# Four seven-product k pairs instead of three in two more FFN column groups, and two sums of squares taken at fixed later steps

## The chip, the cores and the metric

The kernel runs on one core of a Trainium2 chip. The metric is the device time of one execution in microseconds (us); less is better. Engines are called by the profile's names: PE (TensorE matmul), PEld (its weight load), DVE (VectorE), ACT (ScalarE), POOL (GpSimd) and SP (SyncE, which issues most transfers).

## The reference, cut to what matters

A trunk of two pre-norm residual layers over x of 1 x 256 x 2048 in float32. Layer 0 mixes with sliding-window attention and an mLSTM, layer 1 with forgetting attention (FoX); each is followed by the same feed-forward network (FFN) with 5632 hidden columns:

```python
def swiglu(xn, w_gate, w_up, w_down):
    return (jax.nn.silu(xn @ w_gate) * (xn @ w_up)) @ w_down

for layer in range(DEPTH):
    xn = rms_norm(h, norm_mix[layer])
    mix = swa_mlstm_mixer(...) if layer % 2 == 0 else forgetting_attention_mixer(...)
    h = h + mix
    h = h + swiglu(rms_norm(h, norm_ffn[layer]), w_gate[layer], w_up[layer], w_down[layer])
return rms_norm(h, norm_final)
```

The change touches the two products with `w_gate` and `w_up`, in both layers, and the step from layer 0's FFN to layer 1, where `rms_norm` needs the mean of the squares of h.

## The kernel before, in words

**Float32 products.** Every float32 operand is split into a high part (a cast to fp32r) and a low part (the operand less the high part). A product is then three matmuls: high·high, high·low and low·high (`three`, L531). For weights ACT makes the cast and DVE the subtraction: `split_chunk` (L187, L188) for a chunk as it is loaded, 128 x 1024, and `split_plain` (L356, L357) for anything else. The split weights lie in eight slots that are used in turn.

**Tiles.** The 256 rows are two row tiles. k (2048) is walked in eight pairs of 128-row slices, numbered 0 to 7. The 5632 hidden columns are eleven groups (0 to 10) of 512. `ffn` (L637) does groups 0–2, 3–6 and 7–10 (`PARTS`), and after each of these parts the down projection over the hidden columns made so far, in two halves of 1024 output columns (`n0` = 0 and 2).

**Pairs.** `pair_group` (L539) computes one group: gate and up for 512 columns, both row tiles, over the eight k pairs in a given order. There are two kinds of pair. A *plain* pair (kind 0) has 2 matrices x 2 slices x 2 row tiles, 8 products of three matmuls: 24 matmuls. A *seven-product* pair (kind 1) takes the two slices, the two row tiles and the two matrices as a 2 x 2 by 2 x 2 block product and does it with seven block products (as Strassen and Winograd do): 21 matmuls. Its weight sums are made by DVE (L607 to L610, four instructions of 128 x 512) before they are split: one loaded chunk, the second half of the other, and two blocks of sums are cast and subtracted. The matching sums of x are made once per layer and kept: for pairs 1, 3 and 5 in `sx`, for pair 7 (`FOURTH`) in `x4` and in unused parts of xh and xl (`sums_x`, L640).

**Order of pairs.** Most groups use `ORDER`, which makes pairs 1, 3 and 5 seven-product; the groups in `DENSE` use `HEAVY`, which makes 1, 3, 5 and 7 so and begins with one. `DENSE` is (4, 8), in both layers.

**Banks.** PSUM has two sets of four banks. A group's plain sums take one set, the seven products' shared sums (`prods`, four banks) the other, and the next group swaps them. At a group's end `combine` (L553) copies or adds the four prods into c, and L665 adds the four plain banks. So the next group's products wait for L665, and its plain sums for `combine`.

**What sets the order.** The kernel is traced under a scheduler that puts each engine's instructions in an order of its own. Beyond that, a list `todo` ties a job to a step: `run_due` runs it after the weights of the given position of a group have been split.

**Layer 0's end.** The last down projection's second half (`n0` = 2) follows that of `n0` = 0. When an output quarter n of 512 columns is done, `close` (L727) adds it to h (`add_out`, L370, and L758), turns it and splits it into the x of layer 1, and takes its squares. Quarter 0 is turned by DMA: `split_turned` copies it to 16-bit planes in a box (L315), issues four transposes (L317), and its second half, put in `todo` at step 5, copies them back (L322) and scales and splits them (L361 on ACT, L362 on DVE). Quarters 1 to 3 are turned on PE and split likewise. The squares (`square_sum`, L240) are two ACT instructions of 128 x 512 per quarter (L245), and are issued right after a quarter's turn. `r1 = rstd("m1")` needs all of them, at the start of layer 1.

Of the kernel before, what the change touches and what calls it, by code (L numbers as in the profile page):

```python
# [35 lines left out]
ORDER = ((0, 0), (1, 1), (0, 2), (1, 3), (0, 4), (1, 5), (0, 6), (0, 7))  # L36
HEAVY = ((1, 1), (0, 0), (1, 3), (0, 2), (1, 5), (0, 4), (1, 7), (0, 6))
FOURTH = 7
DENSE = (4, 8)
DOWN = {  # L40
    6: ((0, 0), (1, 1), (0, 2), (1, 3), (0, 4), (0, 5)),
    8: ((0, 0), (1, 1), (0, 2), (1, 3), (0, 4), (1, 5), (0, 6), (0, 7)),
# [9 lines left out]
W_RAWS = 4  # L52
LATER = (6, 10, 3, 5)
LATER_DOWN = (5, 6)
RAWS = 4
P_JOIN = 4
COLD = 9
# [18 lines left out]
def trunk(  # L76
# [51 lines left out]
    def load_raw(w, k0, c0, n, pool=wr, bufs=4, raws=None):  # L128
        if raws:
            raw = raws.pop(0)  # L130
            raws.append(raw)
        else:
            raw = pool.tile([P, CK, NB], F32, tag="raw", name="raw", bufs=bufs)
        loaded[0] = nc.sync.dma_start(
            raw[:, :, 0:n], w[k0 * P : (k0 + CK) * P, c0 : c0 + n].rearrange("(k p) n -> p k n", p=P)
        )
        return raw
# [46 lines left out]
    def split_chunk(raw, n):  # L184
        hi, lo = slot()
        for k in (slice(0, 1), slice(1, CK)) if any(raw is f for f in fine) else (slice(0, CK),):
            latest[0] = nc.scalar.copy(hi[:, k, 0:n], raw[:, k, 0:n])  # L187
            nc.vector.tensor_tensor(  # L188
                out=lo[:, k, 0:n], in0=raw[:, k, 0:n], in1=hi[:, k, 0:n].bitcast(F32), op=ALU.subtract
            )  # L190
        return hi, lo
# [48 lines left out]
    def square_sum(key, n):  # L240
        if n == 0:
            sums[key] = sm.tile([P, NT, 4], F32, tag="ss", name="ss")
        for t in range(NT):
            junk = sm.tile([P, NB], BF16, tag="junk", name="junk", bufs=1)
            nc.scalar.activation(  # L245
                junk, h[:, t, n * NB : (n + 1) * NB], AF.Square, accum_out=sums[key][:, t, n : n + 1]
            )
# [34 lines left out]
    def split_scaled(idx, n, extra=None, joined=None):  # L282
        for half in range(2):
            if joined is None:
                pt = pm.tile([P, 2, NT, P], F32, tag="pm", name="pt")
                for i in range(2):
                    k = 4 * n + 2 * half + i
                    for t in range(NT):
                        nc.tensor.transpose(pt[:, i, t, :], h[:, t, k * P : (k + 1) * P], ident)
            else:  # L290
                pt = joined[:, 2 * half : 2 * half + 2, :].rearrange("p i (t q) -> p i t q", t=NT)
            for i in range(2):
                k = 4 * n + 2 * half + i
                src = pt[:, i, :, :].rearrange("p t q -> p (t q)")
                split_gained(xh[:, k, :], xl[:, k, :], src, idx * KT + k)
            pair = 2 * n + half
            if extra is not None and (pair in mixed_of(ORDER) or pair == FOURTH):
                sh, sl, x4, pool = extra

                def copies(full):  # L300
                    for i in range(2):
                        g = gT[:, idx * KT + 2 * pair + i : idx * KT + 2 * pair + i + 1]
                        nc.scalar.mul(full[:, i, :], pt[:, i, :, :].rearrange("p t q -> p (t q)"), g)

                if pair == FOURTH:
                    sums_of(pool, rooms(xh), rooms(xl), copies, x4=x4)
                else:
                    j = mixed_of(ORDER).index(pair)
                    sums_of(pool, sh[:, j, :, :], sl[:, j, :, :], copies)

    def split_turned(idx, n, flat, turned, extra=None):
        planes = flat.bitcast(U16).rearrange("p (b t n) -> p b t n", b=2, t=NT)
        hu = h[:, :, n * NB : (n + 1) * NB].bitcast(U16).rearrange("p t (n b) -> p t n b", b=2)
        for b in range(2):
            nc.scalar.copy(planes[:, b, :, :], hu[:, :, :, b])  # L315
            for t in range(NT):
                nc.sync.dma_start_transpose(turned[:, b, :, t, :], planes[:, b, t, :])  # L317

        def join():
            ju = flat.bitcast(U16).rearrange("p (n b) -> p n b", b=2)  # L320
            for b in range(2):
                nc.scalar.copy(ju[:, :, b], turned[:, b, :, :, :].rearrange("p k t q -> p (k t q)"))  # L322
            split_scaled(idx, n, extra, flat.rearrange("p (k s) -> p k s", k=4))

        return join

    def turn(src, dst):
        planes = dst.rearrange("p k s -> p (k s)").bitcast(U16).rearrange("p (b t n) -> p b t n", b=2, t=NT)
        turned = src.rearrange("p t n -> p (t n)").bitcast(U16).rearrange("p (b k t q) -> p b k t q", b=2, t=NT, q=P)
        su = src.bitcast(U16).rearrange("p t (n b) -> p t n b", b=2)  # L330
        for b in range(2):
            nc.scalar.copy(planes[:, b, :, :], su[:, :, :, b])
        for b in range(2):
            for t in range(NT):
                nc.sync.dma_start_transpose(turned[:, b, :, t, :], planes[:, b, t, :])

        def join():
            du = dst.rearrange("p k s -> p (k s)").bitcast(U16).rearrange("p (n b) -> p n b", b=2)
            for b in range(2):
                nc.scalar.copy(du[:, :, b], turned[:, b, :, :, :].rearrange("p k t q -> p (k t q)"))  # L340

        return join

    def scrap(fp, n):
        if n % 2 == 0:
            box = fp.tile([P, 4, NB], F32, tag="c", name="box", bufs=1)
            halves = box[:, 0:2, :], box[:, 2:4, :]
        elif n == 3:
            halves = [fp.tile([P, 3, NB], F32, tag=f"sd{i}", name="box", bufs=1)[:, 0:CK, :] for i in range(2)]
        else:  # L350
            halves = [fp.tile([P, CK, NB], F32, tag="raw", name="box", bufs=RAWS) for _ in range(2)]
        flat, turned = (a.rearrange("p a n -> p (a n)") for a in halves)
        return flat, turned.bitcast(U16).rearrange("p (b k t q) -> p b k t q", b=2, t=NT, q=P)
# [13 lines left out]
    def add_out(acc, n):  # L367
        for t in range(NT):
            o = h[:, t, n * NB : (n + 1) * NB]
            nc.vector.tensor_tensor(out=o, in0=acc[t], in1=o, op=ALU.add)  # L370
# [165 lines left out]
    def bank(par, name):  # L536
        return pm.tile([P, NB], F32, tag="pm", name=name) if par else pa.tile([P, NB], F32, tag="acc", name=name)

    def pair_group(fp, par, lhs, sums, mats, order, todo=(), halves=None, inner=None, raws=None):  # L539
# [32 lines left out]
        for pos, (kind, pair) in enumerate(order):  # L572
# [21 lines left out]
            if first:  # L594
                prods = [bank(1 - par, "prod") for _ in range(4)]
            ra, rb = (load_raw(w, k0, c0, NB, fp, W_RAWS if halves else RAWS, raws) for w, c0 in mats)
            hg, lg = split_chunk(ra, NB)
# [39 lines left out]
    def ffn(layer, fp, sx, x4, sd, key, todo, idx_next=None, key_next=None, finish=None):  # L637
# [8 lines left out]
        for g0, g1 in zip(PARTS, PARTS[1:]):  # L646
# [3 lines left out]
            for g in range(g0, g1):  # L650
# [6 lines left out]
                    [(w_gate[layer], g * NB), (w_up[layer], g * NB)],  # L657
                    HEAVY if g in DENSE else ORDER,
                    todo,
                )  # L660
                todo = []
# [59 lines left out]
                todo = [(MID if g < g1 - 1 else MID_DOWN, join)]  # L721
# [5 lines left out]
            def close(acc, n):  # L727
                if not end:
                    add_out(acc, n)
                elif idx_next is None:  # L730
                    finish(acc, n, gf)
                else:
                    add_out(acc, n)
                    if n < 1:
                        todo.append((LATER_DOWN[n], split_turned(idx_next, n, *scrap(fp, n))))
                    else:
                        split_scaled(idx_next, n)
                    square_sum(key_next, n)

            gf = None  # L740
            wd = w_down[layer][4 * g0 * P : 4 * g1 * P, :]
            for n0 in (0, 2):
# [9 lines left out]
                todo = []  # L752
# [44 lines left out]
    with tc.tile_pool(name="ev", bufs=1) as ev:  # L797
# [223 lines left out]
        with tc.tile_pool(name="mp", bufs=1) as mp:  # L1021
# [39 lines left out]
            todo = [(AHEAD_M[m], turn(src, dst)) for m, (src, dst) in enumerate(((qm, qmt), (km, kmt)))]  # L1061
# [92 lines left out]
    with tc.tile_pool(name="od", bufs=1) as od:  # L1154
# [56 lines left out]
        def sums_of_x(j, pair):  # L1211
            def make():
                box = od.tile([P, 12, P], F32, tag="tt", name="box")
                sums_of(od, sx[0][:, j, :, :], sx[1][:, j, :, :], whole(xh, xl, pair), box=box)

            return make

        todo = [(p, sums_of_x(j, pair)) for p, j, pair in [(1, 1, 3), (3, 2, 5), (6, 0, 1)]]
# [15 lines left out]
        for i in range(4):  # L1234
# [23 lines left out]
            elif i < 3:  # L1258
                n = NB if i == 1 else VT
# [117 lines left out]
```

## Time and profile before

| what | us |
|---|---|
| median of 3 runs | 2077.42 |
| lowest and highest | 2076.88 and 2078.46 |
| profiled execution | 2078.39 |
| span of the profile | 2076.7 |

The profile is of one execution, with times in us from the start of its span. A row of the timeline gives the start, the duration, the engine, the kernel's line, the operation, what it writes and reads, the shapes, and how many such instructions in a row were merged; what stands in brackets is the engine's idle time before it and the instruction that ended it. A row of the windows gives each engine's busy time in a stretch. Instructions of one engine overlap a little, so that the duration of a row is longer than the distance to the next start. 512 hidden columns take about 41 us in every FFN group, and there are 22 of them.

### The profile page before, as it was taken

To read this page: it belongs to the slowest core of one execution; us is meant where nothing else is said; L and a number is where in the kernel's file an instruction comes from. 1 tells how busy PE (TensorE), PEld (TensorE's weight loads), DVE (VectorE), ACT (ScalarE), POOL (GpSimd) and SP (SyncE) were. 2 spreads that over 40 slices of the span, in tenths; PEclk is the share of its full clock that TensorE was granted. 3 is DMA by queue.
4 is the path that set the end of the run, shared out by engine and by line. 5 is a ranking of instruction groups with operands and counts; after the bars stand their busy time and mean duration, and the time that the engine had idled before them with its cause. 6 is when DMAs were issued, how large, how long until landed. Compare 5 with 4: busy or idle time off the path is not lost.

```text
span 2076.7 us, 26845 instructions
## 1 busy us (share of the span) xinstructions
PE 2064.6 (99%) x9461; PEld 1712.5 (82%) x9461; DVE 1833.4 (88%) x2391; ACT 1379.3 (66%) x1752; POOL 45.8 (2%) x66
## 2 busy tenths in 40 slices
PE   9999999999999999999999999999999999999998
PEld 7878888888888888888888888888888888888887
DVE  6788769999999999999899678689999999999995
ACT  6777678664676656667677676687655677556763
POOL 1010000000000000000000001000000000000000
PEclk9999999999999999999999999999999999999999
DMA  8566577666567666665676766586756667756664
GB/s 290 171 216 190 189 244 239 212 213 197 187 216 236 210 195 220 225 208 185 206 211 210 224 201 181 160 274 209 233 183 214 213 187 231 232 183 203 207 221 149
DMA packets 309574, 434.86 MB, mean 209 GB/s; under 512 B 106412, under 2 KB 114624, under 8 KB 309312
## 3 DMA queue, kind: packets, MB, share of 16 engines
q1 hardware_dynamic: 307088, 426.27, 65.1%
q0 software_dynamic: 1632, 5.80, 0.8%
q8 instruction: 74, 1.21, 0.2%
q10 hardware_dynamic: 720, 1.09, 0.2%
q14 instruction: 60, 0.49, 0.1%
HBM read 408.68 MB, written 2.12 MB: 198 GB/s over the span
## 4 chain that ended last, share of the span: by engine, by line
PE 89%; DVE 4%; DMA 3%; ACT 2%; issue 2%; SPq 0%; POOLq 0%; POOL 0%; ACTq 0%; DVEq 0%
PE acc L532 19%; PE acc L533 19%; PE acc L534 19%; PE acc L223 5%; PE acc L222 5%; PE acc L224 5%; PE prod L532 5%; PE prod L533 5%; PE prod L534 5%; DVE lo L188 1%; DMA raw<-in_w_in_odd_dram 1%; ACT hi L187 1%; DMA raw<-in_w_down_dram 1%; PE p L386 1%; PE po L487 0%
## 5 line engine op out<-in xcount | busy, mean ns | idle before, releaser
L187 ACT CAST hi<-raw 128x1024 fp32r<-128x1024 f32 (+3 forms) x652 | 657.5, 1027 | 406.6 <-PE acc L534 183.3
L188 DVE TENSOR_TENSOR lo<-raw,hi 128x1024 fp32r<-128x1024 f32 (+3 forms) x652 | 767.3, 1195 | 133.7 <-ACT hi L187 130.3
L533 PE MATMUL acc<-lo,xh 128*128 128x512 f32 x1296 | 504.6, 389 | 0.0
L534 PE MATMUL acc<-hi,xl 128*128 128x512 f32 x1296 | 501.7, 389 | 0.0
L532 PE MATMUL acc<-hi,xh 128*128 128x512 f32 x1296 | 487.4, 390 | 0.0
L534 PEld LDWEIGHTS acc<-hi,xl 128*128 128x128 f32 x1296 | 243.3, 188 | 50.5
L533 PEld LDWEIGHTS acc<-lo,xh 128*128 128x128 f32 x1296 | 243.3, 188 | 50.4 <-issue 0.2
L532 PEld LDWEIGHTS acc<-hi,xh 128*128 128x128 f32 x1296 | 243.3, 188 | 50.4 <-issue 0.2
L356 ACT CAST hi<-raw 128x512 fp32r<-128x512 f32 x212 | 172.8, 819 | 83.0 <-PE acc L534 60.0
L357 DVE TENSOR_TENSOR lo<-raw,hi 128x512 fp32r<-128x512 f32 x212 | 198.8, 940 | 6.3 <-ACT hi L356 6.3
L533 PE MATMUL acc<-lo,mh 128*128 128x512 f32 x466 | 180.8, 389 | 0.0
L534 PE MATMUL acc<-hi,ml 128*128 128x512 f32 x466 | 179.7, 389 | 0.0
L532 PE MATMUL acc<-hi,mh 128*128 128x512 f32 x466 | 171.0, 390 | 1.0 <-ACT hi L187 1.0
L356 ACT CAST hi<-t 128x1024 fp32r<-128x1024 f32 x99 | 104.1, 1051 | 69.2 <-PE prod L534 42.2
L357 DVE TENSOR_TENSOR lo<-t,hi 128x1024 fp32r<-128x1024 f32 x99 | 121.2, 1224 | 10.5 <-ACT hi L356 10.2
L223 PE MATMUL acc<-lo,mh 128*128 128x512 f32 (+1 forms) x322 | 126.3, 392 | 0.0
L222 PE MATMUL acc<-hi,mh 128*128 128x512 f32 (+1 forms) x322 | 125.8, 391 | 0.0
L224 PE MATMUL acc<-hi,ml 128*128 128x512 f32 (+1 forms) x322 | 123.7, 391 | 0.0
L532 PEld LDWEIGHTS acc<-hi,mh 128*128 128x128 f32 x466 | 87.3, 188 | 20.5 <-ACT hi L187 2.6
L533 PEld LDWEIGHTS acc<-lo,mh 128*128 128x128 f32 x466 | 87.5, 188 | 18.3 <-DVE lo L188 0.2
L534 PEld LDWEIGHTS acc<-hi,ml 128*128 128x128 f32 x466 | 87.5, 188 | 18.2
L223 PE MATMUL acc<-lo,xh 128*128 128x512 f32 (+3 forms) x288 | 99.9, 347 | 0.2 <-DVE lo L188 0.2
(362 smaller groups left out, 3219.7 us busy)
## 6 DMA issues: line engine op xcount, KB each, us to landing
raw<-in_w_gate_dram SPq DMA_DIRECT2D x176, 512.0 KB, 4.4
raw<-in_w_up_dram SPq DMA_DIRECT2D x176, 512.0 KB, 4.6
raw<-in_w_down_dram SPq DMA_DIRECT2D x176, 512.0 KB, 5.3
raw<-in_w_in_odd_dram SPq DMA_DIRECT2D x88, 512.0 KB, 5.1
raw<-in_w_in_even_dram SPq DMA_DIRECT2D x51, 512.0 KB, 5.2
raw<-in_w_out_even_dram SPq DMA_DIRECT2D x32, 512.0 KB, 5.4
raw<-in_w_out_odd_dram SPq DMA_DIRECT2D x32, 512.0 KB, 4.9
hr<-in_w_in_even_dram SPq DMA_DIRECT2D x12, 512.0 KB, 4.6
```

Source lines behind the costliest of these rows:

```text
L187: latest[0] = nc.scalar.copy(hi[:, k, 0:n], raw[:, k, 0:n])
L188: nc.vector.tensor_tensor(out=lo[:, k, 0:n], in0=raw[:, k, 0:n], in1=hi[:, k, 0:n].bitcast(F32), op=ALU.subtract)
L222: nc.tensor.matmul(o, ah[:, ts], hi, start=(k == 0), stop=False)
L223: nc.tensor.matmul(o, ah[:, ts], lo, start=False, stop=False)
L224: nc.tensor.matmul(o, al[:, ts], hi, start=False, stop=(k == k_all - 1 and cs.stop == n))
L356: nc.scalar.copy(dst_h, src)
L357: nc.vector.tensor_tensor(out=dst_l, in0=src, in1=dst_h.bitcast(F32), op=ALU.subtract)
L386: nc.tensor.matmul(pq[j % 2][:, j // 2, :], q_of(j, b), k_of(j)[:, 0:cols], start=True, stop=True)
L532: nc.tensor.matmul(o, ah, hi, start=start, stop=False)
L533: nc.tensor.matmul(o, ah, lo, start=False, stop=False)
L534: nc.tensor.matmul(o, al, hi, start=False, stop=stop)
```

## The change

`DENSE` takes in groups 5 and 9, so that in both layers groups 4, 5, 8 and 9 have four seven-product pairs and four plain ones, in the order of `HEAVY`. Groups 5 and 9 lose a plain pair 7 and gain a seven-product pair 7; each has six DVE instructions more (one subtraction of 128 x 1024, one of 128 x 512, four sums of 128 x 512), two ACT casts more (128 x 1024 and 128 x 512) and three matmuls fewer. The loads are the same.

At layer 0's end the squares of quarters 0 and 1 are no longer issued at once, but put in `todo` for steps 2 and 6 of the second half of the down projection. Quarters 2 and 3 stay as they were, as does layer 1's end, which has no such sums (`idx_next` is None there).

```diff
-DENSE = (4, 8)
+DENSE = (4, 5, 8, 9)
...
 LATER_DOWN = (5, 6)
+SQUARES = (2, 6)
...
                     else:
                         split_scaled(idx_next, n)
-                    square_sum(key_next, n)
+                    if n < 2:
+                        todo.append((SQUARES[n], lambda: square_sum(key_next, n)))
+                        todo.sort(key=lambda it: it[0])
+                    else:
+                        square_sum(key_next, n)
```

In ACT's order, the first of quarter 0's two squares stays ahead of the box copies, with a weight cast between, and the second follows them; quarter 1's two come after the casts of the following weights. Lines of the changed kernel are one higher than before from L55 on, and five higher after `close`.

## The prediction

> **What bounds the kernel now.** I read the page first: the busy line, the granted clock, the chain that ended last. Its columns are busy time, share of the span and count.
>
> ```profile
> PE 2064.6 (99%) x9461; PEld 1712.5 (82%) x9461; DVE 1833.4 (88%) x2391; ACT 1379.3 (66%) x1752; POOL 45.8 (2%) x66
> ...
> PEclk9999999999999999999999999999999999999999
> ...
> PE 89%; DVE 4%; DMA 3%; ACT 2%; issue 2%; SPq 0%; POOLq 0%; POOL 0%; ACTq 0%; DVEq 0%
> ```
>
> The reader is to see that TensorE has 12 us of a 2077 us span without work, at the full clock in every slice, and that VectorE at 88% is the only other engine near a limit. So two things can move the time: fewer matmuls, or a VectorE that is late for the matmuls left. The shares are averages, so I then cut layer 0's second half into windows at the first matmul of each group. Columns: stretch, length, then busy (count) of PE, PEld, DVE, ACT and POOL, granted clock, DMA share, GB/s.
>
> ```profile
> 552.30:593.10 40.80, 40.80 (x181) 33.79 (x180) 38.55 (x50) 28.60 (x32) 0.00 (x0) 1.00 0.66 213
> 593.10:634.60 41.50, 41.50 (x184) 34.36 (x183) 40.26 (x51) 29.67 (x32) 0.00 (x0) 1.00 0.69 222
> 634.60:676.10 41.50, 41.50 (x185) 34.37 (x184) 39.63 (x50) 27.55 (x30) 0.00 (x0) 1.00 0.63 206
> ...
> 841.40:882.80 41.40, 41.40 (x184) 34.31 (x183) 38.89 (x49) 28.79 (x33) 0.00 (x0) 1.00 0.67 218
> 882.80:924.30 41.50, 41.50 (x184) 34.35 (x184) 40.50 (x52) 28.39 (x31) 0.00 (x0) 1.00 0.65 212
> 924.30:966.00 41.70, 41.70 (x185) 34.53 (x184) 39.77 (x47) 28.73 (x31) 0.00 (x0) 1.00 0.70 225
> 966.00:1010.80 44.80, 43.24 (x193) 34.78 (x192) 40.86 (x55) 28.34 (x44) 0.00 (x0) 1.00 0.46 137
> ```
>
> They are groups 4, 5 and 6, then 9, 10 and both halves of the last down projection. PE is busy for the whole of every group, and only the last window, where layer 0 ends, has matmuls that wait. Group 4, which has four seven-product pairs already, takes 40.80, and group 5 beside it takes 41.50. VectorE leaves only 1 to 2.5 us free in each.
>
> **The change part by part.** (a) *Matmuls.* A seven-product pair is 21 matmuls, a plain pair 24, so each of groups 5 and 9 loses three. The price is the difference of the two rows: 41.50 − 40.80 = 0.70 by edges rounded to 0.1; by pitch, 41.50/183 = 0.2267 us a matmul, so 0.68. Two groups in two layers: **−2.72 us**. This is on the path that sets the end, because PE has no idle time there.
>
> (b) *Casts and sums.* A plain pair has two casts and two subtractions of 128x1024. A seven-product pair has three and one half as wide, and four sums of 512. So VectorE gets one more 1024 subtraction and five more 512 instructions a group, ScalarE one cast of each width. The input sums of pair 7 exist already, since groups 4 and 8 use them.
>
> ```profile
> 970.47 2.36 DVE L188 TENSOR_TENSOR lo<-raw,hi 128x1024 fp32r<-128x1024 f32 x2
> ...
> 975.73 0.70 DVE L609 TENSOR_TENSOR raw<-raw,t 128x512 f32<-128x512 f32 x1
> 976.46 0.69 DVE L610 TENSOR_TENSOR raw<-raw 128x512 f32<-128x512 f32 x1
> ...
> 983.83 0.68 DVE L607 TENSOR_TENSOR t<-raw 128x512 f32<-128x512 f32 x1
> 984.42 0.69 DVE L608 TENSOR_TENSOR t<-raw 128x512 f32<-128x512 f32 x1
> ```
> ```profile
> L187 ACT CAST hi<-raw 128x1024 fp32r<-128x1024 f32 x13 | 13.5, 1053 | 9.0 <-PE acc L534 4.6 <-issue 1.7 <-DMA raw<-in_w_gate_dram 1.4
> ...
> L356 ACT CAST hi<-raw 128x512 fp32r<-128x512 f32 x3 | 1.9, 617 | 0.3 <-PE acc L534 0.3
> ```
>
> Instructions overlap, so I count from start to start. L608 starts 0.59 after L607; I take 0.60. Two subtractions take 2.36 together and one alone 1.23 (the 649.89 row below), so they start 1.13 apart. So 1.13 + 5 × 0.60 = **4.13 us of VectorE** a group. ScalarE's 1.05 + 0.62 lie beside matmuls: it is busy for 29.67 of 41.50. The loads are the same, 973 SP instructions before and after; only their order changes, and at layer 0's end the 272-wide loads, which are needed first, go ahead of some 512-wide ones. POOL's work is unchanged. I cost these at nothing; no matmul in the windows before the last one waits for a transfer.
>
> Group 5 now opens its second product bank at its 49th matmul, 593.1 + 48 × 0.2267 = 604.0. The bank is free after the second of group 4's additions in this row:
>
> ```profile
> 600.79 1.89 DVE L665 TENSOR_TENSOR c<-acc,c 128x512 f32<-128x512 f32 x3
> ```
>
> The first of its three is the second bank's, done by about 601.5: 2.5 us of cover, so nothing as long as VectorE is not later than that.
>
> (c) *What the 4.13 does to the matmuls.* VectorE's 4.13 more and PE's 0.68 less make it 4.81 later against PE, less the idle time that it can fill. The cover is the lead of a written low half over its first matmul. These are the lowest leads that I found, each with the writer and the first reader:
>
> ```profile
> 610.92 2.37 DVE L188 TENSOR_TENSOR lo<-raw,hi 128x1024 fp32r<-128x1024 f32 x2
> ...
> 615.12 0.39 PE L533 MATMUL acc<-lo,xh 128*128 128x512 f32 x1
> ```
> ```profile
> 649.89 1.23 DVE L357 TENSOR_TENSOR lo<-raw,hi 128x1024 fp32r<-128x1024 f32 x1
> ...
> 655.46 0.39 PE L533 MATMUL prod<-lo,sx 128*128 128x512 f32 x1
> ...
> 900.14 2.37 DVE L188 TENSOR_TENSOR lo<-raw,hi 128x1024 fp32r<-128x1024 f32 x2
> ...
> 904.83 0.39 PE L533 MATMUL acc<-lo,xh 128*128 128x512 f32 x1
> ...
> 1711.17 2.37 DVE L188 TENSOR_TENSOR lo<-raw,hi 128x1024 fp32r<-128x1024 f32 x2
> ...
> 1715.73 0.39 PE L533 MATMUL acc<-lo,xh 128*128 128x512 f32 x1
> ```
>
> Of each pair of subtractions the first counts: it ends 1.23 after the row's start. Group 5: 615.12 − 612.15 = 2.97, in mid-group, when about half of the extra work is done. Group 6: the 649.89 row ends at 651.12, 4.34 ahead of 655.46. Group 10: 904.83 − 901.37 = 3.46. Layer 1's group 6: 1715.73 − 1712.40 = 3.33. Against 4.81 that leaves waits of 0.5, 1.35 and 1.5 if no idle is filled, and none if 1.5 is. VectorE's idle is 1.24 in group 5, 1.87 in group 6, 2.51 in group 9. For groups 5/6 of both layers and 9/10 of layer 1 I take a quarter of the worst, 0.35 each: **+1.0** (0 to 2.5: 0.5 and 1.5 for the two group 6, and 0.5 for layer 1's group 10, taken like layer 0's group 6). Layer 0's group 10 runs into (d) and is counted there.
>
> (d) *Layer 0's end.* Here VectorE has no lead. It works without a pause from the row below, 21 rows of the timeline, to the 976.46 row above, which ends at 977.15:
>
> ```profile
> 951.44 0.69 DVE L607 TENSOR_TENSOR t<-raw 128x512 f32<-128x512 f32 x1 [0.91 <-DMA raw<-in_w_down_dram]
> ```
> ```profile
> DVE lo L188 <- ACT hi L187: 2.1, 2, 1.3
> ```
>
> VectorE's idle in the windows of 9, 10 and the first down half is 2.51 + 1.00 + 1.93 = 5.44. The last row above, waits of VectorE from 841.4 to 966 (total, times, longest), is of a kind that stays, as a cast must come first; I leave out 1.8 for it. 3.6 of 4.81 is filled, and layer 0's end comes **+1.2** later (0 to 4.8).
>
> (e) *The squares.* Rows of ScalarE there, two waits of 972 to 993, and the transposes (first and last issue; time to landing):
>
> ```profile
> 973.47 0.63 ACT L245 ACTIVATE junk<-h 128x512 bf16<-128x512 f32 x1 [0.23 <-DVE h L370]
> ...
> 974.66 2.00 ACT L315 COPY box<-h 128x1024 uint16<-128x1024 uint16 x2 [0.47 <-DVE h L370]
> 976.56 0.63 ACT L245 ACTIVATE junk<-h 128x512 bf16<-128x512 f32 x1
> ...
> 977.19 1.03 ACT L187 CAST hi<-raw 128x1024 fp32r<-128x1024 f32 x1
> 978.13 0.62 ACT L245 ACTIVATE junk<-h 128x512 bf16<-128x512 f32 x1
> ...
> 980.21 0.62 ACT L245 ACTIVATE junk<-h 128x512 bf16<-128x512 f32 x1
> ...
> 981.77 0.82 ACT L361 ACTIVATE xh<-pt,gT 128x256 fp32r<-128x256 f32 x2
> 982.49 2.57 ACT L322 COPY box<-box 128x1024 uint16<-128x1024 uint16 x2
> ```
> ```profile
> PEld acc L532 <- ACT hi L187: 1.4, 2, 0.7
> ...
> PE prod L532 <- DVE xl L362: 1.0, 1, 1.0
> ```
> ```profile
> L317 SPq DMA_TRANSPOSE box<-box x4: 1202/1239/1259, 975.7 to 979.6; - x4
> ...
> DMA to landing us min/median/max: 2.4/2.5/2.5
> ```
>
> All four squares stand among the copies and casts that the waiting matmuls need. In the changed order quarter 0's two stay in this stretch; quarter 1's two, 978.13 and 980.21, go behind the casts, 1.25 us off the chain. The 977.19 cast also goes ahead of the box copies and fills the 0.47 pause, so the first L361 could start up to 1.7 sooner (1.25 + 0.47). But that cast takes about 0.9 until its successor starts, 0.4 more than the pause, so the box copies and the transposes come 0.4 later: the last lands at 979.6 + 2.5 + 0.4 = 982.5, where its copy back now starts near 983.7 (the second of the two from 982.49), a gain of 1.2 at most. I take **−1.1** (−1.7 to 0).
>
> Sum: −2.72 + 1.0 + 1.2 − 1.1 = **−1.6 us**. The profiled execution took 2078.39, 1.69 of it around the span, and is 0.97 over the median of the runs, so I take the difference from the median: 2077.42 − 1.6 = **2075.8 us**.
>
> **Rivals.** *R1, VectorE becomes the bound* (the other side: slower). Its place is group 5 to 6, 9 to 10 and layer 0's end; its price 4.81 per group; it decides where the idle isn't filled. With nothing filled, 2.5 + 4.8 = 7.3 comes back against 3.8 saved: 2077.42 + 3.5 = 2080.9. Half of it is the turning point. For it: 40.26 + 4.13 is more than group 5's 40.8. Against: four seven-product pairs in group 4 fit in 38.55, and the groups behind leave idle. If the squares' gain fails with it, 2082.0. *R2, every cover holds:* leads of 3 to 4.3 plus the idle are enough: −2.72 − 1.1 gives 2073.6; with the squares' best, 2073.0. *R3, the squares are worth nothing*, as L362 waits for VectorE, not for ScalarE (the 1.0 row): −2.72 + 2.2 gives 2076.9. That the move is only half made is in (e) already. *R4, the added sums don't overlap:* the four hang on one another, and L610 right behind L609 starts 0.73 later (975.73, 976.46), so 5 × 0.73 + 1.23 = 4.88, 0.75 more at each of four places: 2075.8 + 3.0 = 2078.8. Against it, L607 and L608 start 0.59 apart at 0.68 each. The Trainium skill ("VectorE: DVE Perf Modes", section The DRAIN you can't avoid) states such a rule: the next instruction doesn't start until the pipe is empty, unless it isn't held, when it starts earlier. By the rule R4 would hold; the rows 0.59 apart fit its exception.
>
> **How the numbers follow.** Forecast 0.42, R1 0.25, R2 0.18, R3 0.10, R4 0.05. A measurement of this kernel can tell 0.2%, 4.2 us, from no change: under 2073.3 is faster, over 2081.6 slower. Forecast, R3 and R4 lie within, as does R2 but for its low end (0.08 faster). Of R1, half (0.13) lies over the bound: 0.7 more than its 2080.9, by the squares' failure or one more wait, is enough. Same: 0.79. The range goes from R2's low end, 2073.0, to R1's high end, 2082.0.
>
> **What would show it.** In the changed kernel the windows of groups 5 and 9 take 40.8 us with PE busy throughout, and VectorE's busy time there is some 4 us higher with six instructions more. PE's waits for L188 and L357 in groups 5, 6, 9 and 10: under 1 us in sum for R2, about 1 for the forecast, over 2 for R1. At layer 0's end quarter 1's squares stand behind the first L361, the first of these starts ahead of 981.77 less 1.36, and the last window is near 45; at 48 or more R1 holds. L607 to L610 more than 0.7 apart would show R4. A clock under 1.00, or matmuls waiting for a load, would be outside all of this and make the prediction wrong.

## The result: 10.7 us slower, and the profile after

The changed kernel takes 2087.85 us (median of 4 runs, 2087.45 to 2088.21) against 2077.15 before on the same chip: a ratio of 1.0049, with a 95% interval of 1.0036 to 1.0061. The prediction was 2075.8, with a range up to 2082.0. The profiled execution took 2088.18, its span is 2086.3, 9.6 longer than before.

The busy line of the page, and the windows of layer 0's groups 5, 6, 9, 10 and of the last half of its down projection, cut at the first matmuls of the changed kernel's groups:

```profile
PE 2067.5 (99%) x9449; PEld 1709.8 (82%) x9449; DVE 1849.0 (89%) x2415; ACT 1385.5 (66%) x1760; POOL 42.9 (2%) x66
```
```profile
593.70:636.50 42.80, 41.73 (x182) 33.74 (x181) 41.51 (x52) 29.70 (x33) 0.00 (x0) 1.00 0.70 203
636.50:678.10 41.60, 41.60 (x183) 34.09 (x182) 40.51 (x52) 29.04 (x32) 0.00 (x0) 1.00 0.68 220
843.90:886.20 42.30, 41.63 (x182) 33.81 (x181) 41.25 (x52) 29.22 (x33) 0.00 (x0) 1.00 0.68 203
886.20:929.00 42.80, 42.15 (x184) 34.12 (x183) 41.43 (x53) 29.07 (x32) 0.00 (x0) 1.00 0.68 219
970.40:1017.90 47.50, 44.48 (x194) 36.30 (x194) 42.05 (x54) 30.19 (x48) 0.00 (x0) 0.96 0.47 141
```

The page still says 99% and 89%; it doesn't show what happened. The windows do: group 5 has fewer matmuls and takes 42.8 instead of 41.5, and so it goes in group 10, which the diff doesn't touch. VectorE's busy time grew by 1849.0 − 1833.4 = 15.6, against 16.5 forecast (4 × 4.13).

This table has the length in us of the groups that differ most, start to start of the groups' first matmuls, as in the windows; the columns behind "after" are experiments of the next section. In the kernel of "load" PE's order mixes the end of group 8 with the start of group 9, so group 9 is taken there by its 183 matmuls; edges are good to about 0.3. "Down a" is the first half of the down projection behind groups 6 and 10, "down b" the second half, where layer 0 ends.

| group | before | after | groups alone | sums out | load | third of load | sums out twice |
|---|---|---|---|---|---|---|---|
| layer 0: 5 | 41.5 | 42.8 | 42.9 | 41.5 | 41.5 | 41.5 | 40.8 |
| 6 | 41.5 | 41.6 | 41.6 | 41.3 | 42.8 | 41.5 | 41.5 |
| down a | 41.5 | 42.0 | 42.0 | 41.5 | 45.0 | 45.7 | 41.7 |
| 9 | 41.5 | 42.3 | 42.8 | 41.9 | 41.8 | 41.5 | 40.8 |
| 10 | 41.5 | 42.8 | 42.7 | 41.3 | 43.4 | 41.5 | 41.5 |
| down a | 41.7 | 41.5 | 41.5 | 43.3 | 42.7 | 41.5 | 41.7 |
| down b | 44.8 | 47.5 | 46.5 | 48.3 | 44.4 | 49.6 | 44.7 |
| layer 1: 5 | 41.5 | 43.5 | 43.2 | 41.5 | 41.5 | 41.5 | 40.8 |
| 6 | 41.5 | 41.6 | 41.6 | 41.3 | 43.2 | 41.5 | 41.5 |
| down a | 41.5 | 41.8 | 41.6 | 41.5 | 45.3 | 43.6 | 41.7 |
| 9 | 41.5 | 41.6 | 41.8 | 41.9 | 42.1 | 41.5 | 40.8 |
| 10 | 41.5 | 42.7 | 42.7 | 42.3 | 43.7 | 41.5 | 41.5 |

In the column "after" the rows of groups 5, 6, 9, 10 and down a are 7.5 longer in sum than before, and down b 2.7; 0.6 less is spent in other places. Without any wait groups 5 and 9 would be at 40.8, so the groups hold 7.5 + 2.7 = 10.2 us of new waits, that second 2.7 being the matmuls saved. Of down b's 2.7, by the two windows, 1.5 is idle time of PE (47.50 − 44.48 against 44.80 − 43.24) and 1.2 is busy time, at a granted clock of 0.96.

What PE waits for, in group 5 of layer 0 and of layer 1 (total, times, longest; PEld's waits are those of the weight loads), and the matmul itself:

```profile
PE acc L533 <- ACT c L556: 1.0, 1, 1.0
...
PEld prod L534 <- DVE lo L358: 0.5, 1, 0.5
PEld acc L534 <- DVE lo L189: 0.3, 1, 0.3
```
```profile
PE acc L533 <- ACT c L556: 1.6, 1, 1.6
```
```profile
631.63 0.50 PE L533 MATMUL acc<-hi,xh 128*128 128x512 f32 x1 [1.02 <-ACT c L556]
```

Only 0.5 and 0.3 of it are late low halves (L358 and L189), the kind of wait that I had priced. The longer one is on L556, ScalarE's copy of the first product bank, which frees the bank that the next group's plain sums need. ScalarE's timeline ahead of it:

```profile
625.22 2.00 ACT L188 CAST hi<-raw 128x1024 fp32r<-128x1024 f32 x2 [2.18 <-PE acc L535]
627.12 1.04 ACT L357 CAST hi<-raw 128x1024 fp32r<-128x1024 f32 x1
628.07 2.00 ACT L188 CAST hi<-raw 128x1024 fp32r<-128x1024 f32 x2
629.97 0.61 ACT L357 CAST hi<-raw 128x512 fp32r<-128x512 f32 x1
630.49 0.61 ACT L357 CAST sd<-s 128x512 fp32r<-128x512 f32 x1
631.00 0.57 ACT L556 COPY c<-prod 128x512 f32<-128x512 f32 x1
```

ScalarE waits 2.18 for PE to release a slot, then works through six weight casts and one of sums without a pause, and the copy stands behind them in line. It isn't slow, it is late, at a place where a write of VectorE's is not seen at all. These rows alone don't tie it to VectorE's time; number 11 below does.

Layer 0's end, ScalarE, then PE, then the four transposes (first and last issue):

```profile
979.20 0.63 ACT L246 ACTIVATE junk<-h 128x512 bf16<-128x512 f32 x1 [1.77 <-DVE h L371]
...
980.88 1.06 ACT L188 CAST hi<-raw 128x1024 fp32r<-128x1024 f32 x1 [0.96 <-ACT junk L246]
981.84 1.99 ACT L316 COPY box<-h 128x1024 uint16<-128x1024 uint16 x2
...
986.77 0.82 ACT L362 ACTIVATE xh<-pt,gT 128x256 fp32r<-128x256 f32 x2
989.40 2.52 ACT L323 COPY box<-box 128x1024 uint16<-128x1024 uint16 x2 [1.81 <-issue]
```
```profile
992.92 0.47 PE L533 MATMUL prod<-hi,sd 128*128 128x512 f32 x1 [3.02 <-DVE xl L363]
```
```profile
L318 SPq DMA_TRANSPOSE box<-box x4: 1196/1240/1262, 982.9 to 986.8; - x4
```

The squares of quarter 1 are gone from this stretch. In their place ScalarE is idle for 1.81: the copies back (L323) wait until the last transpose, issued at 986.8 and 2.5 in flight, has landed at 989.3. The weight cast at 980.88 stands ahead of the box copies, and waits 0.96 there. The first transpose is issued 982.9 − 978.48 = 4.4 after the start of VectorE's additions into h, against 975.7 − 972.74 = 3.0 before, so that cast costs the transposes 1.4.

### The profile page after: what moved, and what is told of

The parts are those of the page before. It is cut to its first block, busy times and chain, and to the rows that moved or that the text cites. A ratio compares the mean times of both kernels' runs of the same rounds, so it can differ in the third digit from the quotient of the medians.

```text
span 2086.3 us, 26844 instructions
## 1 busy us (share of the span) xinstructions
PE 2067.5 (99%) x9449; PEld 1709.8 (82%) x9449; DVE 1849.0 (89%) x2415; ACT 1385.5 (66%) x1760; POOL 42.9 (2%) x66
## 3 DMA queue, kind: packets, MB, share of 16 engines
q10 hardware_dynamic: 720, 1.09, 0.1%
## 5 line engine op out<-in xcount | busy, mean ns | idle before, releaser
L189 DVE TENSOR_TENSOR lo<-raw,hi 128x1024 fp32r<-128x1024 f32 (+3 forms) x648 | 762.0, 1191 | 126.7 <-ACT hi L188 123.8
L534 PE MATMUL acc<-lo,xh 128*128 128x512 f32 x1272 | 495.8, 390 | 0.4 <-DVE lo L189 0.4
L535 PE MATMUL acc<-hi,xl 128*128 128x512 f32 x1272 | 493.5, 389 | 0.0
L533 PE MATMUL acc<-hi,xh 128*128 128x512 f32 x1272 | 475.5, 391 | 3.9 <-ACT c L556 2.7
L533 PEld LDWEIGHTS acc<-hi,xh 128*128 128x128 f32 x1272 | 238.7, 188 | 57.1 <-ACT c L556 3.5
L534 PEld LDWEIGHTS acc<-lo,xh 128*128 128x128 f32 x1272 | 238.8, 188 | 50.8 <-DVE lo L189 1.5
L535 PEld LDWEIGHTS acc<-hi,xl 128*128 128x128 f32 x1272 | 238.8, 188 | 49.6
L357 ACT CAST hi<-raw 128x512 fp32r<-128x512 f32 (+1 forms) x220 | 179.1, 819 | 84.1 <-PE acc L535 68.7
L358 DVE TENSOR_TENSOR lo<-raw,hi 128x512 fp32r<-128x512 f32 (+1 forms) x220 | 204.8, 934 | 7.5 <-ACT hi L357 7.4
L358 DVE TENSOR_TENSOR lo<-t,hi 128x1024 fp32r<-128x1024 f32 x103 | 125.5, 1218 | 8.2 <-ACT hi L357 8.2
```

Of the source, the lines that this page charges most:

```text
L189: nc.vector.tensor_tensor(out=lo[:, k, 0:n], in0=raw[:, k, 0:n], in1=hi[:, k, 0:n].bitcast(F32), op=ALU.subtract)
L357: nc.scalar.copy(dst_h, src)
L358: nc.vector.tensor_tensor(out=dst_l, in0=src, in1=dst_h.bitcast(F32), op=ALU.subtract)
L533: nc.tensor.matmul(o, ah, hi, start=start, stop=False)
L534: nc.tensor.matmul(o, ah, lo, start=False, stop=False)
L535: nc.tensor.matmul(o, al, hi, start=False, stop=stop)
```

## The experiments

Theory A: VectorE's added time is the cause, wherever it shows. Theory B: the order of pairs is, with the group's last seven-product pair too close to its end. Rival C: the squares. All kernels but those of a lone square or load are the kernel before with groups 5 and 9 (or 1) in `DENSE`, and all times are medians beside the kernel before on the same chip.

**1. The groups alone.**

```diff
-DENSE = (4, 8)
+DENSE = (4, 5, 8, 9)
```

> Groups 5 and 9 with four seven-product pairs, the squares as in the kernel before. Theory A: VectorE's 4.1 us more a group make its low halves late, and matmuls wait for them; theory B: the order is what costs, as a group that ends with a seven-product pair and one plain pair holds up ScalarE's copy of the products (L555), behind casts that wait for a free slot, and so the next group's first matmuls. Both put the 10.7 us here: 2087 to 2089, the upper end if the later squares gain the 1.1 us that I forecast. Rival C, that the squares cost most: under 2083.

2086.52 against 2077.60, ratio 1.0043 (1.0031 to 1.0056). The loss is in the groups; C falls. The 1.8 us between this and the full change lie within the two intervals. In the two traces, layer 0's last window is 46.5 here and 47.5 after the change.

**2. The later squares alone.**

```diff
+SQUARES = (2, 6)
...
-                    square_sum(key_next, n)
+                    if n < 2:
+                        todo.append((SQUARES[n], lambda: square_sum(key_next, n)))
+                        todo.sort(key=lambda it: it[0])
+                    else:
+                        square_sum(key_next, n)
```

> The later squares alone. A and B: 1.1 us less than before at most and 0 at least, 2076.0 to 2077.2, as no weight cast stands ahead of the box copies here. C: 4 us or more over before, 2081 or above.

2077.82 against 2077.60, ratio 1.0001 (0.9992 to 1.0010): the 1.1 us gain that I forecast is not seen, though the interval (−1.7 to +2.1 us) doesn't exclude it. ScalarE's rows show why there should be none: where the squares stood it now waits for PE, and the copies back start at 982.68, against 982.49 before:

```profile
980.84 1.05 ACT L357 CAST hi<-t 128x1024 fp32r<-128x1024 f32 x1 [0.70 <-PE prod L535]
...
982.68 2.58 ACT L323 COPY box<-box 128x1024 uint16<-128x1024 uint16 x2
```

**3. The groups alone, without pair 7's sums.** The four sums of weights are left out, and both casts take the loaded chunk.

```diff
+            skip = nosum and pair == 7
-            t4 = ra if halves else fp.tile(...)
+            t4 = ra if halves or skip else fp.tile(...)
...
+            if not skip:
                 nc.vector.tensor_tensor(out=ta, ...)
                 ...
...
+                    nosum=g in (5, 9),
```

> As the first, but the four sums of weights (L607 to L610) of pair 7 in groups 5 and 9 are left out, and the chunk itself is cast in their place: 2.4 us of VectorE less in each of four groups, with all casts, subtractions, matmuls and slots kept. A: of the 12.4 us of added waits more than half goes, 2078 to 2082. B: within 2 us of the first kernel, 2086 to 2089.

2083.42 against 2077.60, ratio 1.0027 (1.0016 to 1.0037): 3.1 below the first kernel, between the two forecasts. The table is clearer: most of group 5's and 6's waits are gone in both layers, but down a behind group 10 has a new one, and layer 0's end is at 48.3. So the sums' time on VectorE is at work; the rest of the added work still costs.

**4. VectorE's load alone.** No pair is changed; six additions that nothing needs.

```diff
+        if load_more[0]:  # plain pair 7 of groups 5 and 9
+            nc.vector.tensor_tensor(out=raw[:, 0, 0:n], in0=raw[:, 0, 0:n], in1=raw[:, 1, 0:n], op=ALU.add)
+            nc.vector.tensor_tensor(out=raw[:, 1, 0:n], in0=raw[:, 0, 0:n], in1=raw[:, 1, 0:n], op=ALU.add)
+            nc.vector.tensor_tensor(out=raw[:, 0, 0:n], in0=raw[:, 0, 0:n], in1=raw[:, 1, 0:n], op=ALU.add)
```

> The kernel before with six added additions of 128 x 512 on the split raw chunks of plain pair 7 in groups 5 and 9: 3.6 us of VectorE a group that nothing needs, the orders of pairs as before. A: 3.6 of lag against 4.8, about three quarters of the waits, 2084 to 2087. B: under 2 us more than before, 2077 to 2079.

2091.77 against 2077.60, ratio 1.0071 (1.0058 to 1.0083): 14.2 us for 4 × 3.6 = 14.4 us of VectorE. That is above what A expected, without a new pair or a new order of pairs. The longest waits of PE from 634 to 722:

```profile
PE acc L539 <- DVE lo L190: 1.2, 1, 1.2
PE acc L538 <- ACT mh L362: 0.7, 1, 0.7
```

The second is the down projection's wait for the hidden columns of the last group, cast by ScalarE into mh.

**5. The last seven-product pair sooner.**

```diff
+SOONER = ((1, 1), (0, 0), (1, 3), (0, 2), (1, 5), (1, 7), (0, 4), (0, 6))
...
-                    HEAVY if g in DENSE else ORDER,
+                    (SOONER if g in (5, 9) else HEAVY) if g in DENSE else ORDER,
```

> The first kernel (the groups alone) with another order of pairs in groups 5 and 9: both last seven-product pairs one after the other and then two plain pairs, as in the other groups, instead of one. Work as in the first, which took 2086.5. A (VectorE's time): within 1.5 us of it, 2085 to 2088. B (the late copy of the products, L555, which PE waited for 1.0 and 1.6 us in the changed kernel): 3 us or more below it, under 2083.5.

2102.55 against 2077.39, ratio 1.0123 (1.0109 to 1.0137). Both forecasts are missed. B's cure works where it was meant to, as group 5 has few waits now (41.2 us), but it adds 16 us, so the late copy isn't the whole cause; and the same work for VectorE, with two seven-product pairs in a row, costs far more than A has it. Some 7 of the 16 are 36 matmuls at half the clock, of which the last section tells. Down a behind group 6 has the longest wait, on mh:

```profile
PE acc L533 <- ACT mh L357: 4.9, 1, 4.9
```
```profile
705.93 1.05 ACT L188 CAST hi<-raw 128x1024 fp32r<-128x1024 f32 x1 [3.05 <-DMA raw<-in_w_down_dram]
706.93 1.36 ACT L705 COPY c<-turned 128x1024 uint16<-128x1024 uint16 x1
...
711.92 1.04 ACT L357 CAST mh<-c 128x1024 fp32r<-128x1024 f32 x1
```

The weight cast that waits 3.05 for its load isn't what held the copies back from their transposes (L705): those transposes are issued from 699.6 to 704.1 and take 3.7 to 6.7 us to land, against 690.1 to 694.0 and 2.4 to 3.7 before. They are late because ScalarE's copies ahead of them start at 698.58 (689.07 before). Two more weight casts, one of which waits 0.55 for its load, then stand between the copies back and the cast of mh.

**6. Pair 7's sums on POOL.** Nothing is left out.

```diff
+            eng = nc.gpsimd if aside and pair == 7 else nc.vector
-            nc.vector.tensor_tensor(out=ta, ...)
+            eng.tensor_tensor(out=ta, ...)
...
+                    aside=g in (5, 9),
```

> The first kernel with the four sums of weights of pair 7 in groups 5 and 9 on POOL instead of VectorE: nothing is left out, VectorE has 2.4 us a group less. A: the waits of groups 5, 6, 9 and 10 fall as they did without the sums, from 8.1 us to about 2.5, as long as POOL's four instructions take less than the time that the chunk lies there; and as no weight cast stands ahead of the box copies here, layer 0's last window is near 45, not 46.5: 2078 to 2081. B: 2085 or more.

2084.37 against 2077.39, ratio 1.0035 (1.0022 to 1.0047). By the ratios 2 us are won over number 1, within the two intervals; the forecast was 5.5 to 8.5. Layer 0's last window is 44.3, as forecast, with no weight cast ahead of the box copies. But POOL is slow with the sums, and the down projections wait for mh again (1.5 us behind layer 0's group 6):

```profile
614.88 4.43 POOL L608 TENSOR_TENSOR t<-raw 128x512 f32<-128x512 f32 x1 [284.63 <-DVE lo L357]
619.28 1.29 POOL L609 TENSOR_TENSOR t<-raw 128x512 f32<-128x512 f32 x1
620.54 1.34 POOL L610 TENSOR_TENSOR raw<-raw,t 128x512 f32<-128x512 f32 x1
621.96 1.82 POOL L611 TENSOR_TENSOR raw<-raw 128x512 f32<-128x512 f32 x1
```

**7. Group 1 instead, with no such group beside it.**

```diff
-DENSE = (4, 8)
+DENSE = (1, 4, 8)
```

> The kernel before with one group more, 1, in both layers, between two groups of the common order, not behind one of the four-pair groups. A: VectorE's 4.1 us a group cost 2 to 2.5 of waits against 0.7 saved, as in groups 5 and 9: 2077.4 + 2 x 1.5 = 2080.5, 2079 to 2082. Rival D, that only neighbours hurt each other: 2077.4 - 1.4 = 2076.

2083.09 against 2077.39, ratio 1.0032 (1.0019 to 1.0045): 5.7 for two groups. D falls, and A's range is missed as well: two lone groups cost more than its 3. Group 1 takes 43.6 and 44.8 in the two layers where 40.8 is the work.

**8. Pair 7's sums on POOL, and the later squares** (the diffs of 6 and 2).

> As the second of this set with the later squares too. If the squares lie beside the wait for the transposes, as they did alone: within 1 us of that one. If they gain once VectorE is no longer late: 1 us below it.

2085.24 against 2077.39, ratio 1.0040 (1.0026 to 1.0053), 0.9 above number 6 and within its interval. No gain of the squares is seen with VectorE less late, either.

**9. A third of the load.** As 4, with one addition a chunk: 1.2 us a group, 4.8 in all.

```diff
+        if load_more[0]:
+            nc.vector.tensor_tensor(out=raw[:, 0, 0:n], in0=raw[:, 0, 0:n], in1=raw[:, 1, 0:n], op=ALU.add)
```

> As the fourth kernel, with two added additions of 128 x 512 in groups 5 and 9 instead of six: 1.2 us of VectorE a group, 4.8 in all. If leads of 3 to 4 us are cover, as my prediction had it, nothing is seen: 2077 to 2078. If VectorE's time passes through one for one (six additions cost 14.2 for 14.4 us): 2081 to 2083.

2086.87 against 2077.78, ratio 1.0044 (1.0031 to 1.0057): 9.1 us, nearly twice what was added, so both forecasts are missed. Some 4 of the 9.1 are 20 matmuls at half the clock after two of the pauses (last section); the other 5 are what "one for one" forecast. The table tells where. Groups 5, 6, 9 and 10 have no wait: there my leads of 3 to 4 us do cover 1.2. The loss is where the groups' results are handed on, in down a (45.7 and 43.6) and at layer 0's end (49.6). Down a behind group 6 in this kernel, ScalarE and PE:

```profile
707.34 1.04 ACT L189 CAST hi<-raw 128x1024 fp32r<-128x1024 f32 x1 [2.59 <-DMA raw<-in_w_down_dram]
708.29 1.04 ACT L360 CAST mh<-c 128x1024 fp32r<-128x1024 f32 x1
```
```profile
709.38 0.79 PE L536 MATMUL acc<-hi,mh 128*128 128x512 f32 x1 [2.47 <-ACT mh L360]
```

And before:

```profile
699.16 1.05 ACT L356 CAST mh<-c 128x1024 fp32r<-128x1024 f32 x1
703.02 2.00 ACT L187 CAST hi<-raw 128x1024 fp32r<-128x1024 f32 x2 [2.81 <-DMA raw<-in_w_down_dram]
```

Before, ScalarE made mh first and then waited 2.81 for a load, which cost nothing. Here a cast that waits 2.59 for its load has come to stand ahead of the cast of mh, and PE waits 2.47. That load is late for the same reason. SyncE issues it at 702.16, behind the four transposes of this group (696.2 on); before, the loads go on at 695.4, behind transposes from 690.1 on. The transposes follow ScalarE's copies of c, and these follow VectorE's last product for c (L676, L669 before). In this kernel, then before:

```profile
691.10 0.75 DVE L676 SCALAR_TENSOR_TENSOR c<-c,r 128x512 f32<-128x512 f32 x1
695.15 1.99 ACT L704 COPY c<-c 128x1024 uint16<-128x1024 uint16 x2
```
```profile
687.80 0.75 DVE L669 SCALAR_TENSOR_TENSOR c<-c,r 128x512 f32<-128x512 f32 x1
689.07 1.99 ACT L697 COPY c<-c 128x1024 uint16<-128x1024 uint16 x2
```

VectorE is 3.3 us later there, ScalarE's copies, behind more casts, 6.1, and SyncE's loads 6.8.

**10. ScalarE's load alone.**

```diff
+        if load_more[0]:
+            nc.scalar.copy(raw[:, 0, 0:n], raw[:, 1, 0:n])
+            nc.scalar.copy(raw[:, 0, 0:n], raw[:, 1, 0:n])
```

> The kernel before with four added copies of 128 x 512 on ScalarE in groups 5 and 9, 2.1 us a group, where the change adds 1.5. A (VectorE alone is the bound): within 1.5 us of before, 2076 to 2079. Rival E, that the casts, in one line with the copies that PE waits for, are the bound: 2080 to 2086.

2076.21 against 2077.78, ratio 0.9992 (0.9983 to 1.0001): no loss for 2.1 us a group, in spite of ScalarE's part in the waits. E falls. This kernel also keeps the raw chunks longer: its last copy on one ends at 630.8 in layer 0's group 5, number 9's last addition at 628.7 and number 4's at 637.6. So a later release of them isn't what cost in number 9; for number 4 that isn't excluded.

**11. Without the sums of pairs 5 and 7.**

```diff
-            skip = nosum and pair == 7
+            skip = nosum and pair in (5, 7)
```

> The groups alone, with the four sums of pair 7 and also those of pair 5 left out in groups 5 and 9: VectorE has 0.7 us a group less than in the kernel before, as much as PE saves, while casts, slots, order and the late last seven-product pair stay as in the first kernel. A: the three matmuls a group show, 2074 to 2077. B or E: 2081 or more, as without the sums of pair 7 (2083.4).

2073.58 against 2077.78, ratio 0.9981 (0.9972 to 0.9990). With VectorE's time back at its old level, less the 0.7 that PE saves, every wait in the groups is gone. Groups 5 and 9 of layer 0:

```profile
592.90:633.70 40.80, 40.80 (x181) 33.78 (x180) 37.95 (x46) 29.26 (x33) 0.00 (x0) 1.00 0.75 220
839.70:880.50 40.80, 40.80 (x181) 33.78 (x181) 39.42 (x48) 29.00 (x33) 0.00 (x0) 1.00 0.71 227
```

The slots, casts, matmuls and order of pairs are those of the first kernel. So neither the order (B) nor the casts (E) cost anything by themselves: the same change with no time added to VectorE gains its 2.7 us or a little more (2.1 to 5.8 by the interval). What this kernel alone can't part is VectorE's time from the casts' wait for its sums, which is left out with them; numbers 4 and 9 add time alone, and cost about as much as they add or more. Together they show A.

**12. The sums of pairs 5 and 7 on POOL** (number 6 with `pair in (5, 7)`).

> The groups alone, with the sums of pairs 5 and 7 of groups 5 and 9 on POOL: the kernel of before in its work on VectorE but for 0.7 us a group less, as where these sums were left out (2073.6), and nothing is left out. If VectorE's time is all: 2074 to 2077, a version faster than both. But with pair 7 alone on POOL its four sums took 614.88 to 623.8, 9 us against 2.4 on VectorE, and the casts behind them came late (2084.4): if that lateness decides, 2082 or more.

2102.02 against 2077.19, ratio 1.0117 (1.0101 to 1.0134). The second forecast is met. VectorE's own instructions take longer beside POOL as well (last section), and the two aren't separated here. Pair 7's sums in group 5, and PE's longest wait there:

```profile
616.12 2.22 POOL L608 TENSOR_TENSOR t<-raw 128x512 f32<-128x512 f32 x1 [5.70 <-DVE lo L357]
618.30 2.27 POOL L609 TENSOR_TENSOR t<-raw 128x512 f32<-128x512 f32 x1
```
```profile
PE prod L533 <- DVE lo L357: 3.1, 1, 3.1
```

No kernel here that computes everything is shown to beat the one before.

## Why the prediction was wrong, point by point

The added VectorE time and what it cost, with the matmuls' saving taken out of the measured difference:

| kernel | added to VectorE, us | cost, us | of it at half the clock, us (estimate) |
|---|---|---|---|
| third of load (9) | 4 × 1.2 = 4.8 | 9.1 | 4.0 |
| sums out (3) | 16.5 − 9.6 = 6.9 | 5.8 + 2.7 = 8.5 | 1.6 |
| group 1 (7) | 2 × 4.13 = 8.3 | 5.7 + 1.4 = 7.1 | 1.4 |
| load (4) | 14.4 | 14.2 | 0 |
| groups alone (1) | 16.5 | 8.9 + 2.7 = 11.6 | 0 |
| sums out twice (11) | 16.5 − 19.2 = −2.7 | −4.2 + 2.7 = −1.5 | 0 |

The last column is estimated from each profiled execution: in stretches with a granted clock of 0.50 matmuls start 0.43 us apart instead of 0.23, and there are 20 of them in number 9, 8 in number 3 and 7 in number 7. Without it a microsecond added to VectorE costs 0.7 to 1.1 (5.7 for 8.3 in number 7, 5.1 for 4.8 in number 9). The forecast for the groups alone was 2.2 for 16.5.

- **(a), the matmuls: right.** Groups 5 and 9 take 40.8 in number 11, as group 4 does. The 2.72 us are real and are given back several times over.
- **(b), VectorE's 4.13 us and ScalarE's free time: right.** 15.6 us in the trace against 16.5, and number 10 shows ScalarE's share to cost nothing.
- **(c), the step that failed.** "The cover is the lead of a written low half over its first matmul", and a quarter of the worst lead as the price: 1.0 us, at most 2.5. The groups and down a had 10.2 us of new waits. Two things were wrong. First, the low halves are not all that VectorE's lateness passes through. A group also ends through VectorE's additions and ScalarE's copy (L555), which free the banks, and a part through the cast of mh, which the down projection needs. I read no lead at these two places. Number 9 separates them: 1.2 us a group is covered in the groups, and costs 9.1 at the handovers, the clock's part included. Second, I let VectorE's late time be filled from its idle time, and ScalarE's queue be as it was. A different VectorE time gives a different order, and in line behind a cast that waits for a slot or a load the same copy or cast costs microseconds (number 9, and L556 after the change). Which of the two queues a given wait comes from was read from rows, not shown by a run of its own.
- **(d), layer 0's end 1.2 us later: right in size.** VectorE's additions into h start 972.74 − 966.0 = 6.7 us into that window before, and 978.48 − 970.4 = 8.1 after, 1.4 later. (d) and (e) together put this window at +0.1, and it is +2.7: the cast ahead of the box copies and the lower clock come on top. The rows, before and after:

```profile
972.74 2.49 DVE L370 TENSOR_TENSOR h<-acc,h 128x512 f32<-128x512 f32 x4
```
```profile
978.48 2.48 DVE L371 TENSOR_TENSOR h<-acc,h 128x512 f32<-128x512 f32 x4
```

- **(e), the squares worth 1.1 us: wrong, about 0.** I let the first copy back start when its own half had landed. Both wait for all four transposes, which is seen after the change, where ScalarE idles until 989.40 and the last transpose lands at 986.8 + 2.5 = 989.3. Before, that is 979.6 + 2.5 = 982.1, and the first copy began at 982.49. So the squares lay beside a transfer, and taking them away only shows that wait. The cast ahead of the box copies, which I priced at a 0.4 us delay, cost 1.4. It comes with VectorE's added time, not with the squares: the kernels of numbers 1 and 9 have it too, and that of number 2 doesn't.
- **The rivals.** R1 was the right one, in sign and in the engine that it names, and too cheap: 4.6 us at the most, against 10.7. Its argument in favour, that 40.26 + 4.13 is more than 40.8, was the one to follow. Its argument against, that four seven-product pairs in group 4 fit, holds only where the groups around leave VectorE time, and number 7 shows that group 1 has none. R2 fell. R3's claim on the squares holds, for another reason than the one given there. R4 fell: after the change L608 and L609 start 0.60 apart (638.67 and 639.27):

```profile
638.67 0.69 DVE L608 TENSOR_TENSOR t<-raw 128x512 f32<-128x512 f32 x1
639.27 0.69 DVE L609 TENSOR_TENSOR t<-raw 128x512 f32<-128x512 f32 x1
```

- **The signs.** The waits for late low halves in groups 5, 6, 9 and 10, by PEld's, come to 2.3, just over the 2 that I had set for R1; the last window, at 47.5, stays under its 48. A clock under 1.00, which I had put outside of all this, did come, in that window (0.96): it followed a pause that the change had lengthened, so it was a cost to count and not an outside event.

## What to carry to other kernels

Where PE has no idle time in a stage and VectorE only 1 to 2.5 us of 41, as here, price a microsecond added to VectorE at about a microsecond, until a run with only that load shows less, and add the lower clock after each pause that it makes. Read the leads where a stage hands its result on (bank releases, casts of the next stage's input), not only those of the operands in its midst, and look at what stands ahead of these instructions in their engine's line. Before taking work off a chain, find what the next instruction waits for without it: here, a transfer.

## What the runs showed of the hardware

The clock drops after pauses shorter than I would have counted with, and not after each of the same length. After PE's wait of 3.02 us at layer 0's end (the 992.92 row) the granted clock is 0.58 for 4 us, and 12 matmuls run where 18 do in the kernel of number 1, whose wait there was 2.93. In number 9, whose PE waits only 2.47 for mh, it is 0.50. The three stretches, in this order:

```profile
994.00:998.00 4.00, 4.00 (x12) 3.16 (x11) 4.00 (x7) 4.00 (x6) 0.00 (x0) 0.58 0.02 6
```
```profile
994.00:998.00 4.00, 4.00 (x18) 3.06 (x17) 4.00 (x6) 4.00 (x6) 0.00 (x0) 1.00 0.00 2
```
```profile
709.30:710.50 1.20, 1.12 (x3) 0.93 (x4) 1.20 (x2) 1.20 (x3) 0.00 (x0) 0.50 1.05 408
```

In such a stretch matmuls start 0.43 us apart instead of 0.23. It is 3.4 us long after the change (994.0 to 997.4) and at 709.0 in number 9, and 6.8 us long at 992.3 in number 9, and holds 7 to 13 matmuls there: at 0.2 us more each, a pause after which the clock drops costs an estimated 1.4 to 2.6 us beyond itself.

The Trainium skill ("TensorE: Matmul & The Clock Gate", section What's actually happening) has the clock halve after an idle window of about 3.4 us that runs freely. That it hangs on where the pause lies agrees with these rows; that a pause of 2.5 us is enough doesn't follow from a window of that length.

POOL took 1.3 to 4.4 us for an addition of 128 x 512 that VectorE starts every 0.60 us. VectorE is slower beside it, too: an addition of 128 x 128 takes 1.09 us while POOL computes in number 6, and 0.28 after POOL has ended.

```profile
619.63 1.09 DVE L272 TENSOR_TENSOR s<-c 128x128 f32<-128x128 f32 x1 [1.48 <-ACT c L706]
...
624.99 0.28 DVE L275 TENSOR_TENSOR s<-c,s 128x128 f32<-128x128 f32 x1
```
